# Attention's statistics: whole-tile transposition one slot later, and stores from ScalarE's transfer queue

## The chip, the cores and the metric

The kernel runs on one core of a Trainium2 chip. The metric is the device time of one execution in microseconds, as the median of the runs. A program of one core has its five engines: TensorE (PE in the profile; its weight loads are PEld), VectorE (DVE), ScalarE (ACT), GpSimd (POOL) and SyncE (SP), whose queue issues the transfers (SPq).

## The reference

Two layers of a decoder trunk, for 1024 positions of 1024 channels in float32. Layer 0 mixes by dilated attention, layer 1 by a gated linear recurrence; each mixer and each MLP after it closes with a layer norm of `alpha * x + y`. The change is in the attention alone:

```
for (window, dilation) in ((128,1), (512,4), (2048,16)):      # three groups g, 16 heads of 64
    q, k = rotary(proj[g, 0]), rotary(proj[g, 1])
    s = q k^T / 8 inside the dilated window;  m = max(s);  p = exp(s - m);  l = sum(p)
    o_g = (p / l) v;   lse_g = m + log(l)
o = sum over g of softmax(lse)_g * o_g;   y = o @ w_out
```

So each group leaves an output and two statistics, m and l, for each position and head, and the three groups are mixed with weights made of these.

## The kernel before

Heads go in eight pairs `pr` (two heads of 64 rows fill 128 partitions), and the 24 units (pair, group) in twelve `groups` of two: the first unit `a = 0`, the second `a = 1`. The projections of a group are 21 products (`product(n)`, twelve matmuls `pmm` in float32 parts, lines 666 to 668), and the work of the units before is laid between them by hand: `fill[slot]` holds what is called behind product `slot`, and the tables `ROPES`, `OFFS`, `STATS` and `MIX` give the slots, counted from `base`. Inside this stage the order of TensorE and VectorE is that of the code (`in_order`); ScalarE's and SyncE's order is made by the scheduler, from the same sequence. After the last product the rest goes as `lists` into the output projection (`outproj_ln`), where a scheduler orders all engines: there L183 to L185 are its matmuls on `aoh`, `aol` (the split attention output) and `woh`, `wol` (the split weights, loaded as `wor`); attention outputs of earlier pairs were spilled to DRAM and come back as `onr`.

A unit's core has six steps, two slots apart: `qk` (scores `s`; VectorE adds the mask and takes the row maximum, ScalarE the exponential `p` with its sum), `vtrans` (`vpt`, copied to `vn`), `ptr` (transposes `ppt` of `p`, copied to `pts`) and `pv` (output bank `o`, copied to `og`). The banks of PSUM: three `mm` for products, two `s`, two `pt` for `vpt`, `ppt`, `mpt` and `fb` in turn, one `o`.

Each unit's maxima and sums go into a tile `stats` of 128 x 32 (statistic, head, block of 128 queries). `combine_tr` has three steps, at the slots of `STATS`: TensorE transposes that tile (`mpt`, L564) and ScalarE copies the 32 rows out (`sr`, L566); SyncE stores them in DRAM (`mdram`, L569); SyncE loads them back into `ml` in the layout in which the three groups meet (L575 for dilation 1, L578 otherwise). When a pair's last group, dilation 1, is there, `combine` makes the weights (`mn`, `ml`, L592 to L609), split into `fh` and `fl`, and sends them with six transfers into six rows of `frow` (L616); `combine_mul` spreads them over the partitions with a matmul (`fb`, L626) and VectorE multiplies `og` by it (L627) and adds the groups (L629, L630).

Of the kernel before, what the change touches and what calls it, by code (L numbers as in the profile page):

```python
# [9 lines left out]
F32 = mybir.dt.float32  # L10
F32R = mybir.dt.float32r
U8 = mybir.dt.uint8
AF = mybir.ActivationFunctionType
# [3 lines left out]
P = 128  # L17
# [5 lines left out]
DIL = (1, 4, 16)  # L23
# [29 lines left out]
RESIDENT = 2  # L53
MIX = ((20, 21, 21, 24, 25, 30, 31, 32, 33, 33, 34, 35, 35, 36),
       (30, 31, 33, 34, 35, 37, 38, 39, 41, 41, 42, 42, 42, 43))
STATS = ((12, 13, 15), (21, 22, 24))
ROPES = ((-5, -3, -3, -1, 1, 2), (5, 7, 7, 9, 11, 11))
ROPES0 = ((-5, -2, -1, 2), (-4, 0, 1, 4))
OFFS = ((1, 3, 5, 7, 9, 11), (10, 12, 14, 16, 18, 20))
# [3 lines left out]
def trunk_kernel(  # L63
# [24 lines left out]
    nc = tc.nc  # L88
    cp = ctx.enter_context(tc.tile_pool(name="cp", bufs=1))
# [6 lines left out]
    def U(name, dt=F32):  # L96
        return up.tile([P, 1024], dt, name=name, tag="u")

    def bank(tag, name):
        return ps.tile([P, 512], F32, name=name, tag=tag, bufs={"mm": 3, "s": 2, "pt": 2, "o": 1}[tag])  # L100

    def small(shape, name, bufs=4, dt=F32):
        return sp.tile(shape, dt, name=name, tag=name, bufs=bufs)

    act = nc.scalar.activation
# [21 lines left out]
    ident = cp.tile([P, P], F32, name="ident")  # L127
# [194 lines left out]
    def attention(pre, hc):  # L322
# [120 lines left out]
        sel = cp.tile([P, NG * P], F32R, name="bsel")  # L443
        frow = U("frow", F32R)
        mdram = dp.tile([NPAIR, NG, 2, 2, S], F32, name="mdram")

        def constants():
            nc.sync.dma_start(cosT, cos_t)
            nc.sync.dma_start(sinT, sin_t)
            nc.sync.dma_start(mask, masks)  # L450
# [11 lines left out]
        def nat(ap, g):  # L462
            d = DIL[g]
            return ap if d == 1 else ap.rearrange("p (n r) -> p n r", r=d)

        def rope(e, g, nm):
            rot = U("rot")
            for b4 in range(4):
                o = (b4 ^ 1) * 32
                nc.sync.dma_start(rot[b4 * 32:b4 * 32 + 32, :], e[o:o + 32, :])  # L470
            qT = U(nm)
            nc.vector.tensor_mul(cls(qT, g), nat(e, g), nat(cosT, g))
            return qT, (lambda: nc.vector.tensor_mul(rot, rot, sinT),
                        lambda: nc.vector.tensor_add(cls(qT, g), cls(qT, g), nat(rot, g)))
# [84 lines left out]
                [lambda: pv(6), lambda: pv(7)],  # L559
            ]  # L560

        def combine_tr(pr, g, sS, ml):
            pt = bank("pt", "mpt")
            nc.tensor.transpose(pt[:32, 0:P], sS.rearrange("p w a b -> p (w a b)"), ident)  # L564
            sr = small([32, P], "sr", 2)
            act(sr, pt[:32, 0:P], AF.Copy)  # L566
            yield
            md = mdram[pr, g]
            nc.sync.dma_start(md.rearrange("w h (b q) -> (w h b) q", q=P), sr)  # L569
            yield  # L570

            d = DIL[g]
            for w in range(2):
                if d == 1:
                    nc.sync.dma_start(ml[:, w, 0, :], md[w].rearrange("h (i n) -> (h i) n", n=P))  # L575
                else:
                    for h in range(2):
                        nc.sync.dma_start(  # L578
                            ml[8 * h:8 * h + 8, w, g, :].rearrange("i (r n) -> i r n", r=d),
                            md[w, h].rearrange("(r i n) -> i r n", r=d, i=8))  # L580
            yield

        def combine(pr, ml):
            def cv(tl, g):
                d = DIL[g]
                return tl if d == 1 else tl.rearrange("p (r n) -> p n r", r=d)

            m = ml[:, 0]
            l = ml[:, 1]
            v = nc.vector  # L590
            mn = small([16, P], "mn", 1)
            v.tensor_tensor(nat(mn, 1), nat(m[:, 0], 1), cv(m[:, 1], 1), op=ALU.min)  # L592
            v.tensor_tensor(nat(mn, 2), nat(mn, 2), cv(m[:, 2], 2), op=ALU.min)
            for g in range(NG):
                v.tensor_sub(cv(m[:, g], g), nat(mn, g), cv(m[:, g], g))
            act(m, m, AF.Exp)
            yield
            v.tensor_mul(l, l, m)
            den = mn
            v.tensor_add(nat(den, 1), nat(l[:, 0], 1), cv(l[:, 1], 1))  # L600
            v.tensor_add(nat(den, 2), nat(den, 2), cv(l[:, 2], 2))
            yield
            v.reciprocal(den, den)
            for g in range(NG):
                v.tensor_mul(nat(l[:, g], g), cv(m[:, g], g), nat(den, g))

            fh = wp.tile([P, 512], F32R, name="fh", tag="p")[:16, :NG * P].rearrange("p (g t) -> p g t", t=P)
            fl = wp.tile([P, 512], F32R, name="fl", tag="pts")[:16, :NG * P].rearrange("p (g t) -> p g t", t=P)
            act(fh, l, AF.Copy)  # L609
            yield  # L610
            v.tensor_sub(fl, l, fh.bitcast(F32))
            yield
            for g in range(NG):
                for i, f in enumerate((fh, fl)):
                    r = 4 * g + 2 * i
                    nc.sync.dma_start(frow[r:r + 2, :].bitcast(F32).rearrange("h (i t) -> h i t", t=P),  # L616
                                      f[:, g, :].bitcast(F32))
            yield

        def combine_mul(pr, og, hb):  # L620

            c = slice(hb * 512, hb * 512 + 512)
            acc = og[0]
            for g in GORD:
                fb = bank("pt", "fb")
                nc.tensor.matmul(fb, sel[:, g * P:(g + 1) * P], frow[:, c], start=True, stop=True)  # L626
                nc.vector.tensor_mul(og[g][:, c], og[g][:, c], fb)  # L627
                yield
            nc.vector.tensor_add(og[2][:, c], og[2][:, c], og[1][:, c])  # L629
            nc.vector.tensor_add(acc[:, c], acc[:, c], og[2][:, c])  # L630
            yield
            if hb:
                if pr < SPILL[0]:
                    nc.sync.dma_start(ond[0, pr], acc)
                    oN.append(ond[0, pr])
                else:
                    oN.append(acc)
            yield
# [4 lines left out]
        def at(slot, f):  # L643
            fill.setdefault(slot, []).append(f)

        ep, acc, part = {}, {}, {}
        ml, ogs = {}, {}
# [58 lines left out]
        def unit_work(gi, a, base):  # L706

            pr, g = groups[gi][a]
            if pr not in ml:
                ml[pr] = small([16, 2, NG, P], "ml", 1)  # L710
                ogs[pr] = [None] * NG
            sS = small([P, 2, 2, 8], "stats", 3)

            adds = {}

            def rope_of(t):
                res[a, t], adds[t] = rope(ep.pop((gi, a, 0 if t == 1 else 1)), g, "qT" if t == 0 else "kT")

            def begin():
                ogs[pr][g] = U("og")  # L720
                p = pieces(pr, g, res.pop((a, 0)), res.pop((a, 1)), ep.pop((gi, 2, a)), ogs[pr][g], sS)
                for f in p[0]:
                    f()
                work.extend(p[1:])

            work = []
            later = [lambda: [f() for f in work.pop(0)] for _ in range(5)]
            trs = combine_tr(pr, g, sS, ml[pr])
            stats = [lambda: next(trs, None)] * 3
            mix = []  # L730
            if g == GORD[-1]:
                steps = combine(pr, ml[pr])
                mix = [lambda: next(steps, None)] * 5
                for hb in range(2):
                    muls = combine_mul(pr, ogs[pr], hb)
                    mix += [lambda muls=muls: next(muls, None)] * (4 + hb)
            return adds, rope_of, [begin] + later, stats, mix
# [23 lines left out]
        for n in range(len(seq)):  # L761
            gi, i, j = seq[n]
# [26 lines left out]
            if n % 21 == 14:  # L789
# [3 lines left out]
                for a in range(2):  # L793
                    adds, rope_of, core, stats, mix = work[a]
# [9 lines left out]
                    for k, f in enumerate(core):  # L804
                        at(base + UNIT0 + OFFS[a][k], f)
                    for k, f in zip(STATS[a], stats):
                        at(base + k, f)
# [9 lines left out]
        (ra, ca, sa, _), (rb, cb, sb_, mx) = tail  # L817
        done = [f for n in sorted(fill) for f in fill[n]]
        mine = [[ra[0]], [rb[0], rb[1]], [ra[1]], [ca[0], rb[2]], [ca[1]], [cb[0]], [ca[2]], [cb[1]], [ca[3]], [cb[2]],
                [ca[4]] + sa, [cb[3]], [ca[5]], [cb[4]] + sb_, [cb[5]], mx[:1], mx[1:3], mx[3:5], [],  # L820
                mx[5:7], mx[7:10], mx[10:]]
        lists = [done[k:k + 1] + (mine[k] if k < len(mine) else []) for k in range(max(len(done), len(mine)))]
        return oN, lists
# [661 lines left out]
    def hgrn(xs, late, consts, pre, gw):  # L1485
# [103 lines left out]
        for hd in range(8):  # L1589
# [66 lines left out]
            if hd == 0:  # L1656
                new = [[]] + new
            pend = [(pend[i] if i < len(pend) else []) + (new[i] if i < len(new) else [])
                    for i in range(max(len(new), len(pend)))]
# [9 lines left out]
    pr = Out(w_attn_out, "a", 0)  # L1669
    hc = []  # L1670
    oN, fill = attention(pr.pre_steps, hc)
    xf, late = outproj_ln(pr, oN, fill, lambda t: x[t * P:(t + 1) * P, :],
                          ln_mix_g[0], ln_mix_b[0], x1d)
# [3 lines left out]
    pr = Out(w_hgrn_out, "h", 1)  # L1677
# [81 lines left out]
```

## Time and profile before

| | us |
|---|---|
| median of 3 runs | 2845.02 (2842.76 to 2846.17) |
| the profiled execution | 2844.54 |
| its span, first to last instruction | 2842.8 |
| TensorE busy | 2772.0 |
| VectorE busy | 2068.6 |
| ScalarE busy | 1449.2 |
| mean granted clock of TensorE | 0.996 |

In a row of a timeline stand start, duration, engine, line, operation, tile written and tiles read, and in brackets how long the engine was idle before it and what ended that. Matmuls overlap, so the price of one in TensorE's stream is the distance from its start to the next start, not its duration. In a row of waits stand the total, the number and the longest one. In a row of a tile's instructions stand the least, median and greatest duration in ns. Attention's products run from about 14 to 970 us, the rest of its units until about 1065 us, inside the output projection.

### The profile page before, as it was taken

Reading aid. Unit: us, or ns where it says so; the run is one execution under the profiler, and the core shown is the slowest. Engines: PE = TensorE matmul, PEld = TensorE weight load, DVE = VectorE, ACT = ScalarE, POOL = GpSimd, SP = SyncE. Lnnn points to the kernel's source line nnn. Section 1 sums busy time; section 2 is a strip of 40 time slices with the busy share of each in tenths; the row PEclk is TensorE's granted clock in tenths of the full one; section 3 lists DMA queues with packets and bytes.
Section 4 is the critical chain, followed back from the end, with each engine's and each line's share of the span. In section 5 each row is a group of like instructions: output and inputs, shape, how many; then the busy total and the mean of one; then the engine's idle time right before and its main releaser. Section 6 shows DMA issues by size and latency. Waiting matters only on the chain. (4 is left out here: it accounts for less than half of the span.)

```text
span 2842.8 us, 40144 instructions
## 1 busy us (share of the span) xinstructions
PE 2772.0 (98%) x14280; PEld 2229.9 (78%) x14280; DVE 2068.6 (73%) x3830; ACT 1449.2 (51%) x3105; POOL 122.7 (4%) x67
## 2 busy tenths in 40 slices
PE   8999999999999989999999999999999999999998
PEld 6777777777777767888878887787787788878887
DVE  7768777777777767786686876565667787678677
ACT  5555555555555555544454434555553545454433
POOL 0000000000000003100000011111102200000000
PEclk9999999999999999999999999999999999999999
DMA  7766665766667523464494752101132455475654
GB/s 288 252 200 195 185 206 172 216 198 206 193 194 219 166 87 133 145 226 156 158 320 126 263 177 90 38 31 60 55 117 81 149 204 174 159 271 189 222 175 132
DMA packets 204936, 485.27 MB, mean 171 GB/s; under 512 B 29376, under 2 KB 43712, under 8 KB 204736
## 3 DMA queue, kind: packets, MB, share of 16 engines
q1 hardware_dynamic: 204736, 482.72, 51.5%
q8 instruction: 112, 1.84, 0.3%
q14 instruction: 88, 0.72, 0.1%
HBM read 362.82 MB, written 94.24 MB: 161 GB/s over the span
## 5 line engine op out<-in xcount | busy, mean ns | idle before, releaser
L666 PE MATMUL pmm<-xh,H 128*128 128x512 f32 x1008 | 407.6, 404 | 13.0 <-ACT H L432 8.9
L668 PE MATMUL pmm<-xh,H 128*128 128x512 f32 x1008 | 395.7, 393 | 0.1
L667 PE MATMUL pmm<-xl,H 128*128 128x512 f32 x1008 | 395.6, 392 | 0.0
L666 PEld LDWEIGHTS pmm<-xh,H 128*128 128x128 f32 x1008 | 190.9, 189 | 53.3 <-ACT H L432 8.9
L668 PEld LDWEIGHTS pmm<-xh,H 128*128 128x128 f32 x1008 | 190.2, 189 | 42.3 <-DVE H L440 0.8
L667 PEld LDWEIGHTS pmm<-xl,H 128*128 128x128 f32 x1008 | 191.0, 189 | 36.6
L514 ACT ACTIVATE p<-p,stats 128x128 f32<-128x128 f32 (+1 forms) x384 | 168.3, 441 | 93.6 <-DVE stats L511 92.2
L1260 PE MATMUL pdy<-dT,dS 128*128 128x512 f32 x512 | 199.2, 389 | 0.0
L1263 PE MATMUL pdy<-dT,dS 128*128 128x512 f32 x512 | 199.2, 389 | 0.0
L1264 PE MATMUL pdy<-dT,dS 128*128 128x512 f32 x512 | 199.2, 389 | 0.0
L511 DVE CUSTOM_DVE_ANT_0 p<-s,mask 128x128 f32<-128x128 f32 (+1 forms) x384 | 113.3, 348 | 67.7 <-PE s L500 58.4
L137 ACT ACTIVATE dS<-dr 128x512 fp32r<-128x512 f32 x192 | 119.5, 622 | 73.2 <-PE pdy L1264 36.6
L171 PE MATMUL pmm<-f0nh,wh 128*128 128x512 f32 x384 | 153.2, 399 | 0.0
L173 PE MATMUL pmm<-f0nh,wl 128*128 128x512 f32 x384 | 149.9, 390 | 1.6 <-DVE wl L138 1.6
L172 PE MATMUL pmm<-f0nl,wh 128*128 128x512 f32 x384 | 149.7, 390 | 0.0
L138 DVE TENSOR_TENSOR dS<-dr,dS 128x512 fp32r<-128x512 f32 x192 | 136.2, 710 | 15.8 <-ACT dS L137 13.9
L214 POOL TENSOR_TENSOR z<-z,bB 128x1024 f32<-128x1024 f32 x24 | 58.5, 2442 | 1680.8 <-ACT z L213 1676.7
L527 ACT ACTIVATE pts<-ppt 128x256 f32<-128x256 f32 (+1 forms) x192 | 85.4, 474 | 62.0 <-PE ppt L524 59.8
L137 ACT ACTIVATE dT<-hold 128x512 fp32r<-128x512 f32 x128 | 80.0, 625 | 69.9 <-DVE hold L1239 28.8
L1073 ACT ACTIVATE H<-wc 128x512 fp32r<-128x512 f32 x128 | 77.2, 625 | 73.5 <-DVE wc L1066 44.0
L1263 PEld LDWEIGHTS pdy<-dT,dS 128*128 128x128 f32 x512 | 96.1, 188 | 20.1
L1260 PEld LDWEIGHTS pdy<-dT,dS 128*128 128x128 f32 x512 | 96.1, 188 | 19.8
(395 smaller groups left out, 6950.3 us busy)
## 6 DMA issues: line engine op xcount, KB each, us to landing
xh<-xtd SPq DMA_DIRECT2D x110, 512.0 KB
xl<-xtd SPq DMA_DIRECT2D x110, 512.0 KB
dr<-hd SPq DMA_DIRECT2D x192, 256.0 KB
dr<-in_w_down_dram SPq DMA_DIRECT2D x128, 256.0 KB
rot<-e SPq DMA_DIRECT2D x192, 128.0 KB
wa<-in_w_up_dram SPq DMA_DIRECT2D x48, 512.0 KB
wb<-in_w_attn_dram SPq DMA_DIRECT2D x36, 512.0 KB
wa<-in_w_attn_dram SPq DMA_DIRECT2D x33, 512.0 KB
```

Source lines behind the costliest of these rows:

```text
L137: act(hi, raw, AF.Copy)
L138: nc.vector.tensor_sub(lo, raw, hi.bitcast(F32))
L171: nc.tensor.matmul(o, wh[:, k], xs.h(k), start=k == 0, stop=False)
L172: nc.tensor.matmul(o, wh[:, k], xs.l(k), start=False, stop=False)
L173: nc.tensor.matmul(o, wl[:, k], xs.h(k), start=False, stop=k == NK - 1)
L514: act(p[:, h, :n], p[:, h, :n], AF.Exp, bias=sS[:, 0, h, b:b + 1], scale=-1.0, accum_out=sS[:, 1, h, b:b + 1])
L666: nc.tensor.matmul(o, wh, hi[k // 2][:, c], start=begin and k == 0, stop=False, skip_group_check=True)
L667: nc.tensor.matmul(o, wh, lo[k // 2][:, c], start=False, stop=False, skip_group_check=True)
L668: nc.tensor.matmul(o, wl, hi[k // 2][:, c], start=False, stop=end and k == 3, skip_group_check=True)
L1260: nc.tensor.matmul(o[q], h, T_[:, L], start=begin, stop=False, skip_group_check=True)
L1263: nc.tensor.matmul(o[q], h, T_[:, R], start=False, stop=False, skip_group_check=True)
L1264: nc.tensor.matmul(o[q], l, T_[:, L], start=False, stop=end, skip_group_check=True)
```

## The change

`stats` becomes one tile of 128 x 128 for the whole run, with four slots of 32 columns that the units use in turn; GpSimd clears it once. `combine_tr` transposes the whole tile (128 columns in place of 32) and copies the 32 rows of its slot, at partitions `q0` and up. The three steps are one slot later in `STATS`, and in the lists behind the last product the first step has a place of its own, the other two stand one list later (unit b's first step one place earlier in its list). The store comes from ScalarE's transfer queue. For dilation 1 two transfers go from `sr` straight into `ml`, and nothing goes to DRAM; for the other two groups the loads into `ml` stay with SyncE. Of the six rows of `frow`, the three of `fh` are issued by ScalarE, the three of `fl` by SyncE.

```diff
-STATS = ((12, 13, 15), (21, 22, 24))
+STATS = ((13, 14, 16), (22, 23, 25))
...
+        allS = cp.tile([P, P], F32, name="stats")
+        nc.gpsimd.memset(allS, 0.0)
...
-        def combine_tr(pr, g, sS, ml):
+        def combine_tr(pr, g, slot, ml):
             pt = bank("pt", "mpt")
-            nc.tensor.transpose(pt[:32, 0:P], sS.rearrange("p w a b -> p (w a b)"), ident)
-            sr = small([32, P], "sr", 2)
-            act(sr, pt[:32, 0:P], AF.Copy)
+            nc.tensor.transpose(pt[:, 0:P], allS, ident)
+            q0 = slot * 32
+            sr = small([P, P], "sr", 2)
+            act(sr[q0:q0 + 32], pt[q0:q0 + 32, 0:P], AF.Copy)
             yield
             md = mdram[pr, g]
-            nc.sync.dma_start(md.rearrange("w h (b q) -> (w h b) q", q=P), sr)
+            d = DIL[g]
+            if d == 1:
+                for w in range(2):
+                    nc.scalar.dma_start(ml[:, w, 0, :], sr[q0 + 16 * w:q0 + 16 * w + 16])
+            else:
+                nc.scalar.dma_start(md.rearrange("w h (b q) -> (w h b) q", q=P), sr[q0:q0 + 32])
             yield
 
-            d = DIL[g]
-            for w in range(2):
-                if d == 1:
-                    nc.sync.dma_start(ml[:, w, 0, :], md[w].rearrange("h (i n) -> (h i) n", n=P))
-                else:
+            if d > 1:
+                for w in range(2):
                     for h in range(2):
                         nc.sync.dma_start(
...
-                for i, f in enumerate((fh, fl)):
+                for i, (f, eng) in enumerate(((fh, nc.scalar), (fl, nc.sync))):
                     r = 4 * g + 2 * i
-                    nc.sync.dma_start(frow[r:r + 2, :].bitcast(F32).rearrange("h (i t) -> h i t", t=P),
-                                      f[:, g, :].bitcast(F32))
+                    eng.dma_start(frow[r:r + 2, :].bitcast(F32).rearrange("h (i t) -> h i t", t=P),
+                                  f[:, g, :].bitcast(F32))
...
-            sS = small([P, 2, 2, 8], "stats", 3)
+            slot = (2 * gi + a) % 4
+            sS = allS[:, slot * 32:slot * 32 + 32].rearrange("p (w a b) -> p w a b", w=2, a=2)
...
-                [ca[4]] + sa, [cb[3]], [ca[5]], [cb[4]] + sb_, [cb[5]], mx[:1], mx[1:3], mx[3:5], [],
+                [ca[4]] + sa[:1], sa[1:] + [cb[3]], [ca[5]], sb_[:1] + [cb[4]], sb_[1:] + [cb[5]], mx[:1], mx[1:3], mx[3:5], [],
```

The lines of the changed kernel are two to nine higher than before: `mpt` is L566, `sr` L569, the direct transfer L575, the store L577, `frow` L621, `fb` L631.

On TensorE, around the transposition of a first unit (pair 0, dilation 1), before:

```order
L668 MATMUL pmm<-xh,H 128x512
L539 MATMUL o<-pts,vn 64x128 x8
L524 MATMUL ppt<-ident,p 128x128 x8
L564 MATMUL mpt<-ident,stats 32x128
L666 MATMUL pmm<-xh,H 128x512
```

and now, twelve `pmm` rows further on:

```order
L673 MATMUL pmm<-xh,H 128x512
L566 MATMUL mpt<-ident,stats 128x128
L502 MATMUL s<-kT,qT 128x128 x4
L490 MATMUL vpt<-ident,vT 128x128 x8
L671 MATMUL pmm<-xh,H 128x512
```

The transposition has moved from behind the unit's last `ppt` to behind the next product, where the second unit's scores and `vpt` follow it.

On ScalarE at the same place, before (`e` is a product's copy, `H` a weight's):

```order
L527 ACTIVATE pts<-ppt 128x512 x2
L566 ACTIVATE sr<-mpt 32x128
L697 ACTIVATE e<-pmm 128x512
L514 ACTIVATE p,stats<-p,stats 128x128 x4
L489 ACTIVATE vn<-vpt 128x512 x2
L432 ACTIVATE H<-wc 128x512
L547 ACTIVATE og<-o 128x512
```

and now:

```order
L529 ACTIVATE pts<-ppt 128x512 x2
L702 ACTIVATE e<-pmm 128x512
L569 ACTIVATE sr<-mpt 32x128
L575 DMA ml<-sr 16x128
L516 ACTIVATE p,stats<-p,stats 128x128 x4
L491 ACTIVATE vn<-vpt 128x512 x2
L432 ACTIVATE H<-wc 128x512
L575 DMA ml<-sr 16x128
L549 ACTIVATE og<-o 128x512
```

The copy `sr` stands behind the next product's copy, and the two issues stand ahead of the exponentials and of `og`. Where a pair's weights go out (the next group's second unit), ScalarE now has:

```order
L614 ACTIVATE fh<-ml 16x384
L569 ACTIVATE sr<-mpt 32x128
L621 DMA frow<-fh 2x8x128
L694 ACTIVATE e<-pmm 128x512
L577 DMA mdram<-sr 32x128
L621 DMA frow<-fh 2x8x128
L432 ACTIVATE H<-wc 128x512
L552 ACTIVATE og<-o 128x8x64
L621 DMA frow<-fh 2x8x128
```

Four issues stand there among the copies; before there was none.

On VectorE, at the end of attention (last pair; `wol` and `aol` are low parts of the output projection's operands), before:

```order
L138 TENSOR_TENSOR aol<-onr,aoh 128x512
L629 TENSOR_TENSOR og<-og 128x512
L630 TENSOR_TENSOR og<-og 128x512
L138 TENSOR_TENSOR wol<-wor,woh 128x512 x2
L592 TENSOR_TENSOR mn<-ml 16x128
L593 TENSOR_TENSOR mn<-mn,ml 16x128
L595 TENSOR_TENSOR ml<-mn,ml 16x128
L595 TENSOR_TENSOR ml<-mn,ml 16x32x4
L595 TENSOR_TENSOR ml<-mn,ml 16x8x16
```

and now:

```order
L597 TENSOR_TENSOR mn<-ml 16x128
L634 TENSOR_TENSOR og<-og 128x512
L138 TENSOR_TENSOR aol<-onr,aoh 128x512
L632 TENSOR_TENSOR og<-og,fb 128x512
L598 TENSOR_TENSOR mn<-mn,ml 16x128
L635 TENSOR_TENSOR og<-og 128x512
L600 TENSOR_TENSOR ml<-mn,ml 16x128
L138 TENSOR_TENSOR wol<-wor,woh 128x512
L600 TENSOR_TENSOR ml<-mn,ml 16x32x4
L138 TENSOR_TENSOR wol<-wor,woh 128x512
L600 TENSOR_TENSOR ml<-mn,ml 16x8x16
```

The first step on `ml` has moved ahead of the adds of the pair before, and the others are mixed with the `wol` steps, the last still behind both.

More of the change, by code (lines that the diff above doesn't have):

```diff
@@ L727, in unit_work @@
             later = [lambda: [f() for f in work.pop(0)] for _ in range(5)]
-            trs = combine_tr(pr, g, sS, ml[pr])
+            trs = combine_tr(pr, g, slot, ml[pr])
             stats = [lambda: next(trs, None)] * 3
```

## The prediction

> **What bounds the kernel now.** I read the page first, then the waits of TensorE (PE), then the timeline around each instruction that the diff moves, then the end of the attention stage on all queues.
>
> ```profile
> span 2842.8 us, 40144 instructions
> PE 2772.0 (98%) x14280; PEld 2229.9 (78%) x14280; DVE 2068.6 (73%) x3830; ACT 1449.2 (51%) x3105; POOL 122.7 (4%) x67
> ```
>
> TensorE is busy for 98% of the span; only its own instruction time, or the 70.8 us in which it isn't busy, can shorten the run. VectorE (DVE) and ScalarE (ACT) matter only where TensorE waits for them. In the waits of TensorE between 90 and 1000 us, which is the attention stage, two rows belong to the transposition that the diff moves (`mpt`), and one row of SyncE's queue to the store behind it:
>
> ```profile
> PE mpt L564 <- ACT pts L527: 3.5, 13, 0.3
> PE mpt L564 <- DVE og L627: 1.4, 3, 0.5
> SPq L569 <- ACT sr L566: 149.5, 21, 13.7
> ```
>
> So 4.9 us of the stage's idle time stand before `mpt`: it needs one of the two `pt` banks, and ScalarE hasn't emptied the one before. No wait of TensorE in this window is for a transfer, so SyncE's 149.5 us behind `sr` cost nothing there.
>
> **Part 1: the transposition one slot later.** The price of a thing in TensorE's stream is best read from start to start. The first, one typical and the last of the 21 transpositions between 120 and 945 us, then the same numbers of transposes (four, eight) with a product right behind them and no `mpt`, then the one `mpt` that already stands behind a product:
>
> ```profile
> 119.09 1.11 PE L524 MATMUL ppt<-ident,p 128*128 128x128 f32 x4
> 120.25 0.40 PE L564 MATMUL mpt<-ident,stats 128*32 128x128 f32 x1
> 120.30 0.78 PE L666 MATMUL pmm<-xh,H 128*128 128x512 f32 x1
> ...
> 236.77 0.66 PE L524 MATMUL ppt<-ident,p 128*128 128x128 f32 x4
> 237.69 0.28 PE L564 MATMUL mpt<-ident,stats 128*32 128x128 f32 x1 [0.26 <-ACT pts L527]
> 237.73 0.49 PE L666 MATMUL pmm<-xh,H 128*128 128x512 f32 x1
> ...
> 942.67 1.09 PE L524 MATMUL ppt<-ident,p 128*128 128x128 f32 x8
> 944.01 0.28 PE L564 MATMUL mpt<-ident,stats 128*32 128x128 f32 x1 [0.25 <-ACT pts L527]
> 944.05 0.49 PE L666 MATMUL pmm<-xh,H 128*128 128x512 f32 x1
> ```
> ```profile
> 110.26 0.66 PE L524 MATMUL ppt<-ident,p 128*128 128x128 f32 x4
> 110.68 0.48 PE L666 MATMUL pmm<-xh,H 128*128 128x512 f32 x1
> ...
> 207.10 1.09 PE L488 MATMUL vpt<-ident,vT 128*128 128x128 f32 x8
> 207.94 0.48 PE L666 MATMUL pmm<-xh,H 128*128 128x512 f32 x1
> ...
> 981.46 0.39 PE L185 MATMUL pmm<-woh,aol 128*128 128x512 f32 x1
> 981.69 0.27 PE L564 MATMUL mpt<-ident,stats 128*32 128x128 f32 x1
> 981.80 0.60 PE L488 MATMUL vpt<-ident,vT 128*128 128x128 f32 x4
> ```
>
> Four transposes lead to the product after 0.42 us without `mpt` and 0.96 with it; eight after 0.84 and 1.38: the step costs 0.54 us. Over the 21, worked out so: seven behind eight transposes 0.54 to 0.60 (4.0 together), six behind four 0.54 (3.3), three with the VectorE wait 0.74 (2.2), three that met no wait 0.11 (0.3), the first two 0.80 and 0.33 (1.1). Sum 10.9 us. In the order the step now stands behind the twelve matmuls of a product, as at 981.69, where it costs 0.11 us. By then the banks have had a product's time, some 2.8 us, to be emptied. 21 x 0.11 = 2.3 us. Bounds of one: 0.11, and 0.54 if the wait comes along. I take 0.11, since that row is the same step in the same kind of place. **Net -8.6 us.**
>
> The transposition reads the whole 128x128 tile, so it waits for the last statistics of all units written ahead of it; one slot after a unit's last exponentials these are done, and the order shows it waiting only for a `pts` copy. Its weight load has 128 columns, not 32; the eight transposes above load 128 too, at 0.105 us each, so this is in the 0.11.
>
> **What is late next.** Where the step is a first unit's, the second unit's `vpt` transposes follow, and their second four now need the bank that `sr` empties.
>
> ```profile
> 206.13 0.39 PE L668 MATMUL pmm<-xh,H 128*128 128x512 f32 x1
> ...
> 206.56 0.60 ACT L697 ACTIVATE e<-pmm 128x512 f32<-128x512 f32 x1 [2.51 <-PE pmm L668]
> ```
>
> ScalarE copies `e` at 206.56 to 207.16, then `sr` (0.27 us, below) to about 207.45. The second four would start at 207.10 + 0.11 + 0.42 = 207.63. It fits, by 0.2 us, so zero; one more copy of 0.6 us ahead of `sr` would cost 0.4 us at each of 11 places, 4.4 us: the upper bound.
>
> **Part 2: transfers issued by ScalarE.** 16 stores to `mdram`, 16 direct ones into `ml` and 24 of `frow`. The trace has no transfer issued by ScalarE; SyncE's are the nearest rows:
>
> ```profile
> L566 ACT ACTIVATE sr<-mpt x24: 249/267/270, 120.7 to 1039.8; 32x128 f32<-32x128 f32 x24
> L569 SPq DMA_DIRECT2D mdram<-sr x24: 317/328/1198, 121.0 to 1040.0; - x24
> L575 SPq DMA_DIRECT2D ml<-mdram x16: 312/375/418, 205.5 to 1041.9; - x16
> L616 SPq DMA_DIRECT2D frow<-fh x24: 610/626/712, 242.4 to 1055.5; - x24
> ```
>
> 16 x 0.328 + 16 x 0.375 + 24 x 0.626 = 26.3 us on ScalarE's queue, in which exponentials, `pts`, `e`, `og` and `H` copies stand behind them. It is busy 51% of the time, and what follows the bursts (four issues, 2.2 us, in slots 22 to 26) is an `og` copy whose bank TensorE wants back six slots later, and copies for products two slots off. So nearly all lies beside TensorE's work. Bounds: 0 and 26.3 us; I take +1.0, near the lower end, since the evictions that TensorE waits for closely (`pts`) don't follow a burst in the order. Each issue also waits for an older transfer on its semaphore; all that I followed back were issued a slot or more before. SyncE loses 56 issues and the waits for `sr`: worth nothing, as no TensorE wait there is for a transfer.
>
> The Trainium skill (DMA: Bandwidth & Descriptors, "Issuing engines are not separate DMA queues") says that issuing from several engines saves only the sequencer's issue time, usually small beside the transfer. By it the move would be worth nothing; the sum has a loss of 1.0 instead, from ScalarE's own queue.
>
> **Part 3: the end of attention.** Here a chain counts: the last unit's statistics, the factors, `fb`, `og`, the output projection.
>
> ```profile
> 1044.18 0.39 PE L185 MATMUL pmm<-woh,aol 128*128 128x512 f32 x1
> 1048.16 0.79 PE L183 MATMUL pmm<-woh,aoh 128*128 128x512 f32 x1 [3.59 <-ACT aoh L137]
> 1048.75 0.63 PE L184 MATMUL pmm<-wol,aoh 128*128 128x512 f32 x1
> ...
> 1054.30 0.40 PE L185 MATMUL pmm<-woh,aol 128*128 128x512 f32 x1
> ...
> 1058.28 0.70 PE L626 MATMUL fb<-frow,bsel 128*128 128x512 f32 x2 [0.83 <-DMA frow<-fh]
> ```
> ```profile
> 1046.16 0.87 DVE L595 TENSOR_TENSOR ml<-mn,ml 16x128 f32<-16x128 f32 x3
> ```
> ```profile
> 1047.07 0.52 ACT L596 ACTIVATE ml<-ml 16x384 f32<-16x384 f32 x1 [0.36 <-DMA onr<-ond]
> 1047.50 0.61 ACT L137 ACTIVATE aoh<-og 128x512 fp32r<-128x512 f32 x1
> ```
> ```profile
> 1041.49 0.79 SPq L575 DMA_DIRECT2D ml<-mdram  x2
> ...
> 1052.41 0.63 SPq L616 DMA_DIRECT2D frow<-fh  x1
> ...
> 1056.17 0.61 SPq L616 DMA_DIRECT2D frow<-fl  x1
> ```
>
> TensorE stops for 3.59 us and then runs 13 matmuls 0.427 us apart ((1054.30 - 1048.75)/13) where 0.23 is usual (981.46 to 981.69): 2.5 us more. The stop ends with `aoh<-og`, which on ScalarE stands behind the exponential of `ml`, and that behind VectorE's L595. The change lets `ml` land earlier (issued at about 1038 for 1041.49), but in the new order VectorE does the same two `og` products, two adds, `aol`, two `wol` and `mn` steps ahead of that exponential, and ScalarE has one `aoh<-onr` copy (0.6 us) more between it and `aoh<-og`. I walk it to about 1047.5 against 1048.16: -0.6 us. After it `frow` goes out on two queues, three by three; the six in a row take 1056.17 + 0.61 - 1052.41 = 4.4 us, half is 2.2, of which the later start of the `fl` rows and two `aol` steps that now stand behind `fb` take most back: another -0.4. **-1.0 us**, between +3 (VectorE held by a late `ml`) and -6.1 (stop and slow clock both gone).
>
> **Sum**, against the profiled execution's 2844.54 us: 2844.5 - 8.6 + 1.0 - 1.0 = 2835.9. The median of the runs is 2845.02, 0.5 above; so 2836 us, -0.3%.
>
> **Rivals.**
> (a) The stop at 1044 us goes, and with it the slow clock: -6.1 in place of -1.0, 2831 us. For it: the `wor`, `onr` and `ml` transfers that ScalarE waited for come sooner. Against: VectorE's chain. The Trainium skill (TensorE: Matmul & The Clock Gate, "HAM oscillation") names idle gaps over some 3.4 us as what halves TensorE's clock; the trace agrees (3.59 us, then 0.427 us), so by it a stop that gets only 0.2 us shorter would already save the 2.5 us.
> (b) Half the gain comes back as waits for banks or for ScalarE (`vpt` behind `sr`, 4.4 us): 2841 us, within 0.2% of before.
> (c) Slower: ScalarE stalls at an issue until an older transfer has landed, and `pts` and the exponentials are late for the next transposes. It costs time once ScalarE is over two slots late, and turns the sum at 14.3/22 = 0.65 us of new TensorE wait for each unit (8.6 lost, 5.7 more for 0.2%); SyncE's single waits reach 13.7 us, so a stuck one could. About 2852 us. Against: the older transfers lie well back.
> (d) The step isn't later at all: the order excludes it.
>
> **Chances.** Forecast 0.50, (a) 0.15, (b) 0.26, (c) 0.09. A measurement of this kernel tells 0.2% (5.7 us) from no change: the forecast and (a) are faster, 0.65; (b) the same, 0.26; (c) slower, 0.09. From 2829.5 (below (a)) to 2844 (past (b)) lies over 8 in 10.
>
> **What would show it.** Right: no `mpt` row among TensorE's waits, `mpt` 0.11 us behind the last matmul of a product, the stage some 8 us shorter by 1000 us. Part 1 wrong: waits of `vpt` for `sr`. Part 2 wrong: TensorE's waits for `pts`, `e` or `og` grow, or ScalarE idles behind transfers. Part 3 wrong: a stop near 1040 us under 3 us, or over 5.

## The result and the profile after

| | before | after |
|---|---|---|
| median, nine runs each on the same chip (us) | 2845.84 (2842.29 to 2846.41) | 2835.93 (2833.36 to 2837.94) |
| the profiled execution (us) | 2844.54 | 2833.53 |
| its span (us) | 2842.8 | 2831.5 |

The changed kernel takes 0.9967 of the time, 95% interval 0.9958 to 0.9976: 9.9 us less. The forecast was 2836.0 us.

The page after, its line of engines (us busy, share of the span, instructions):

```profile
PE 2765.8 (98%) x14280; PEld 2228.6 (79%) x14280; DVE 2068.7 (73%) x3830; ACT 1450.0 (51%) x3105; POOL 122.9 (4%) x68
```

The instruction counts of TensorE, VectorE and ScalarE are those of before. TensorE still sets the time, so the gain has to be stream time and waits of TensorE. Its waits after, between 90 and 985 us (total, number, longest):

```profile
PE ppt L526 <- DVE og L632: 3.0, 6, 0.8
PE ppt L526 <- ACT pts L529: 2.8, 6, 0.5
PE o L541 <- ACT og L552: 2.1, 1, 2.1
PE pmm L183 <- DVE vT L706: 0.8, 1, 0.8
```

These rows stand in the profile before with the same numbers. The two `mpt` rows that stood among them (3.5 and 1.4 us) are gone, and no new row has come.

The transposition in its new place, a first unit's and a second unit's, from the timeline of TensorE:

```profile
203.99 0.39 PE L673 MATMUL pmm<-xh,H 128*128 128x512 f32 x1
204.22 0.27 PE L566 MATMUL mpt<-ident,stats 128*128 128x128 f32 x1
204.42 0.72 PE L502 MATMUL s<-kT,qT 64*128 64x128 f32 x8
...
237.79 0.39 PE L673 MATMUL pmm<-xh,H 128*128 128x512 f32 x1
238.02 0.27 PE L566 MATMUL mpt<-ident,stats 128*128 128x128 f32 x1
238.05 0.48 PE L671 MATMUL pmm<-xh,H 128*128 128x512 f32 x1
238.37 0.39 PE L672 MATMUL pmm<-xl,H 128*128 128x512 f32 x1
```

It starts 0.23 us behind the last matmul of the product, with no bracket for a wait. From that matmul to the other unit's `s` it is 0.43 us (0.32 without a transposition, 206.13 to 206.45 in the trace before), and to the next product 0.26, where two matmuls of a product stand 0.23 apart. The second matmul of that product comes another 0.32 us later, again in place of 0.23, so the price at a second unit's place is spread over two distances.

The difference of the two profiled executions, 11.0 us, put together from distances between marks that both have:

| from, to | before | after | change |
|---|---|---|---|
| start to the first wait for `og`, near 118 us | 118.5 | 118.7 | +0.2 |
| to the first product on `aoh` | 855.4 | 846.1 | -9.3 |
| to the first `lnpt` (end of attention) | 111.9 | 111.6 | -0.3 |
| to the first `hpt` of layer 1 | 711.5 | 710.0 | -1.5 |

From there to the last store both take 1042.1 us. The last row isn't the change's work, for no line there was touched, and 1.55 us of the second aren't either: the granted clock fell behind a wait in the profile before and, by chance, not in the one after (last section). In a second profile of the changed kernel (`after_again`) it fell there too, and the second row is 847.7 us: 7.7 less than before. A distance without such a place is that from the second to the twenty-first transposition: 786.79 us before, 779.15 after. That is 7.64 us for 19 of the steps, 0.40 us each. This distance, called the stage below, is the finest ruler of the case: the changed kernel has 779.15 and, profiled again, 779.16 us.

At the end of attention the stop of TensorE is still there, and longer than the 3.59 us of before:

```profile
1033.21 0.39 PE L185 MATMUL pmm<-woh,aol 128*128 128x512 f32 x1
1038.46 0.69 PE L183 MATMUL pmm<-woh,aoh 128*128 128x512 f32 x1 [4.86 <-ACT aoh L137]
...
1040.84 0.80 PE L185 MATMUL pmm<-woh,aol 128*128 128x512 f32 x1 [0.83 <-DVE aol L138]
...
1047.89 0.61 PE L631 MATMUL fb<-frow,bsel 128*128 128x512 f32 x2
```

What was bought is at 1047.89: no wait for `frow`, where before there were 0.83 us. What was paid is at 1040.84: a wait as long for `aol`, which was not there before.

### The profile page after: what moved, and what is told of

The parts are those of the page before. It is cut to its first block, busy times and chain, and to the rows that moved or that the text cites. A ratio compares the mean times of both kernels' runs of the same rounds, so it can differ in the third digit from the quotient of the medians.

```text
span 2831.5 us, 40028 instructions
## 1 busy us (share of the span) xinstructions
PE 2765.8 (98%) x14280; PEld 2228.6 (79%) x14280; DVE 2068.7 (73%) x3830; ACT 1450.0 (51%) x3105; POOL 122.9 (4%) x68
```

## Experiments

Theory T: the place of the transposition in TensorE's stream, and there the wait for a `pt` bank, makes the gain. Rival Q: the transfers make it. Times are medians beside runs of the kernel before on the same chip, with the ratio to these and its 95% interval.

**The later slots alone, in the kernel before.**

```diff
-STATS = ((12, 13, 15), (21, 22, 24))
+STATS = ((13, 14, 16), (22, 23, 25))
```

> The kernel before with the later slots alone (32 columns, all transfers from SyncE through DRAM, the old lists at the end). Theory T (the place of the transposition in TensorE's stream makes the gain): 8 to 10 us below the kernel before, 2836 to 2838 us, and no wait of TensorE for a bank at the transposition. Rival Q (the gain comes from the transfers: ScalarE's queue, the way without DRAM, SyncE's relief): no change, 2845 us.

Measured: 2836.84 us, ratio 0.9970 (0.9959 to 0.9982). The stage takes 779.87 us; what it has over the changed kernel's 779.15 comes at one place, a wait of 0.38 us for a weight (`H`). One table of the diff gives the stage's gain, all but that wait, and Q falls. This kernel transposes 32 columns and the changed one 128: it is 0.53 us ahead of the changed kernel at the first transposition and 0.50 at the tenth, so in the new place the whole tile costs nothing.

**The old slots in the changed kernel** (the table back, all else as changed).

> The changed kernel with the old slots (12, 13, 15 and 21, 22, 24), all else as changed. T: the gain is gone, 2844 to 2847 us, and the rows of the transposition behind pts and og copies are back among TensorE's waits (about 5 us); a 128-column weight load in that place may add up to 0.03 us at each of 21 places, 0.6 us. Q: it stays near 2836 us.

Measured: 2845.25 us, ratio 0.9999 (0.9990 to 1.0007). The waits of TensorE in the stage have their old rows again:

```profile
PE mpt L566 <- ACT pts L529: 3.7, 14, 0.3
...
PE mpt L566 <- DVE og L632: 1.4, 3, 0.5
```

The whole tile can be priced here: this kernel falls behind the one before by 0.33 us from the third transposition to the sixteenth (1.85 to 2.18 us), 0.025 us a place. Without the slots the rest of the change is worth nothing.

**Every transfer back on SyncE** (whole tile, later slots and lists stay).

```diff
-            if d == 1:
-                for w in range(2):
-                    nc.scalar.dma_start(ml[:, w, 0, :], sr[q0 + 16 * w:q0 + 16 * w + 16])
-            else:
-                nc.scalar.dma_start(md.rearrange("w h (b q) -> (w h b) q", q=P), sr[q0:q0 + 32])
+            nc.sync.dma_start(md.rearrange("w h (b q) -> (w h b) q", q=P), sr[q0:q0 + 32])
...
-                for i, (f, eng) in enumerate(((fh, nc.scalar), (fl, nc.sync))):
+                for i, (f, eng) in enumerate(((fh, nc.sync), (fl, nc.sync))):
```

> The changed kernel with every transfer back on SyncE and dilation 1 again through DRAM; whole tile, later slots and the new lists stay. T: as the changed kernel, 2834 to 2838 us; only the end of attention may differ, by 3 us either way. Q: 2845 us. Of the prediction's terms, ScalarE's 56 issues (+1.0 us, bounds 0 to 26.3) would show here as a gain of so much in the stage up to 965 us.

Measured: 2837.3 us, ratio 0.9971 (0.9959 to 0.9982). It stands 1.88 us behind the changed kernel at the first transposition and 1.92 at the tenth: ScalarE's queue costs nothing there and gives nothing. Then one wait for `H` of 0.76 us, at 514.84, makes it 2.99. Four of the twelve profiles have a single wait of this kind (0.38 to 1.30 us), three of them at the same matmul, and neither kernel that is compared has one; these three cost some 0.3 us more than they lasted (0.38 cost 0.7 above), the one of 1.30 us, with the old slots, did not. Why it comes was not tried.

**Four more stores for each unit on ScalarE's queue.**

```diff
+            for x in range(4):
+                nc.scalar.dma_start(xdram[pr, g, x].rearrange("w h (b q) -> (w h b) q", q=P), sr[q0:q0 + 32])
             yield
 
             if d > 1:
```

> The changed kernel with four further stores of sr to DRAM after each of the 24 first ones, all issued by ScalarE: 96 more issues, at 0.314 us each 30 us more on its queue. What they store is not read. If ScalarE's issues are hidden (the prediction took 1.0 of 26.3 us; the changed kernel's stage shows about 0): 0 to 1.5 us over the changed kernel, 2836 to 2837.5 us. Rival C (ScalarE stands behind older transfers at its issues and pts and p come late): over 5.7 us more, up to 30, 2842 to 2866 us, with TensorE's waits for pts and p grown.

Measured: 2835.56 us, ratio 0.9970 (0.9958 to 0.9981). The added issues, by tile (least, median, greatest in ns), and TensorE's waits in the stage:

```profile
L580 ACTq DMA_DIRECT2D xdram<-sr x96: 308/432/1164, 123.0 to 1030.4; - x96
```
```profile
PE ppt L527 <- DVE og L635: 3.0, 6, 0.8
PE ppt L527 <- ACT pts L530: 2.8, 6, 0.5
```

96 x 0.432 = 41 us more on ScalarE's queue, and the stage takes 779.18 us against 779.15. The wait for `pts` is 2.8 us in both. Rival (c) of the prediction had the right place to look and no price there.

**The old slots, with a bank that is free.**

```diff
-STATS = ((13, 14, 16), (22, 23, 25))
+STATS = ((12, 13, 15), (21, 22, 24))
...
-            pt = bank("pt", "mpt")
+            pt = bank("s", "mpt")
```

> The changed kernel with the old slots, but the transposition writes one of the two s banks instead of a pt bank, so that it has no pts or og copy to wait for in its old place; all else as changed. Theory B (of the 0.54 us of the old place, 0.26 is the wait for the bank and about as much the stream that has to fill again; only 0.11 is the transposition): nearly all the gain comes back without the later slot, 2836 to 2839 us, no bank wait at the transposition. Rival P (the place behind the transposes costs 0.5 us whatever the bank): 2844 to 2847 us.

Measured: 2833.04 us, ratio 0.9962 (0.9950 to 0.9975). The stage takes 778.32 us, 0.8 under the changed kernel's. In the old place, behind eight transposes:

```profile
200.56 1.09 PE L526 MATMUL ppt<-ident,p 128*128 128x128 f32 x8
201.49 0.27 PE L566 MATMUL mpt<-ident,stats 128*128 128x128 f32 x1
201.52 0.48 PE L671 MATMUL pmm<-xh,H 128*128 128x512 f32 x1
```

From `ppt` to the product it is 0.96 us, where the kernel before had 1.38 with the transposition and 0.84 without: 0.12 us instead of 0.54. So it was never the place: it was the bank. The wait that the trace gave as 0.26 us cost 0.42 in the distance of starts. Run again beside the changed kernel on one chip:

> The old slots with an s bank once more. Theory B (only the bank wait made the old place dear): within 1.5 us of the changed kernel beside it. If it is 2 us or more below, the old place is the better one once it has a free bank, since the statistics leave a slot earlier and no transposition stands ahead of a second unit's s.

> The changed kernel once more, beside the next two on one chip: 2834 to 2838 us, 0.9958 to 0.9976 of the kernel before. Its profile shows what changes of itself from run to run (the first wait for H near 9 us, the granted clock behind the short stops).

Measured: 2834.58 us (0.9965, 0.9953 to 0.9978) for the s bank, with a stage of 778.32 us again, against 2835.12 us (0.9966, 0.9954 to 0.9978). By the medians the two ways are equal within what can be told, though the stage is 0.8 us shorter with the `s` bank in both of its profiles. No kernel's median here is measurably lower than the changed one's.

**No transposition at all.** ScalarE fills `sr` from a tile of ones, so the three groups are weighted alike, and the weights depend on no statistics.

```diff
-            pt = bank("pt", "mpt")
-            nc.tensor.transpose(pt[:, 0:P], allS, ident)
...
-            act(sr[q0:q0 + 32], pt[q0:q0 + 32, 0:P], AF.Copy)
+            act(sr[q0:q0 + 32].rearrange("p (o c) -> p o c", o=2), onesT[q0:q0 + 32].rearrange("p (o c) -> p o c", o=1).broadcast_to([32, 2, 64]), AF.Copy)
```

> The changed kernel without the 24 transpositions: ScalarE fills sr from a constant tile of ones, so the three groups are weighted alike. What it gains is what the transposition still costs in its new place. T: 21 x 0.02 to 0.11 us, 0.4 to 2.3 us below the changed kernel, 2833.5 to 2835.5 us. Rival H (the price only moved, to the second unit's vpt and s and to the product behind them): 8 to 11 us below, 2825 to 2828 us.

Measured: 2839.9 us, ratio 0.9981 (0.9972 to 0.9990), a miss for both: slower than the changed kernel. The experiment had a side effect. Nothing holds the copies into `sr` back, so the scheduler put nine of them, with stores, into the first 32 us, and ScalarE stands there until each buffer's transfer is through:

```profile
13.44 0.30 ACT L569 ACTIVATE sr<-ones 32x128 f32<-32x128 f32 x1 [4.70 <-DMA mdram<-sr]
...
21.97 0.31 ACT L569 ACTIVATE sr<-ones 32x128 f32<-32x128 f32 x1 [6.57 <-DMA ml<-sr]
```
```profile
PE pmm L671 <- ACT H L432: 27.2, 1, 27.2
```

TensorE's first wait is 27.2 us in place of 9.5, and the first `s` comes 13.8 us late. The parts can still be read. From the first `s` to the first product on `aoh` it takes 875.4 us, with two waits that the changed kernel doesn't have: 0.59 us for `H` and 0.2 for `p`, which cost some 0.9 and 0.6. The changed kernel takes 876.8. So the 21 transpositions still cost about 3 us. Matmul set against matmul around each place, the changed kernel loses 0.11 to 0.17 us at twenty of them and 0.37 at the last, 3.1 us in all; against the kernel before, which has no transposition at these places, the same comparison gives the same numbers. That is above T's 2.3 us, and far below the 8 of H. And from there to the first `lnpt` it takes 103.5 us where the changed kernel has 111.6: with the weights early, the end of attention is 8.1 us shorter. That is about what the chain behind the last statistics costs (three transpositions at the end are missing too).

**The end of attention: the split of pair 6 ahead of the exponential.**

```diff
             nc.vector.tensor_add(acc[:, c], acc[:, c], og[2][:, c])
+            if pr >= SPILL[0] and hb == 0:
+                pre.__self__.raw[pr] = acc
+                pre.__self__.split_k(pr, 0)
             yield
```

(and no second time in the output projection)

> The changed kernel with one thing moved at the end of attention: the split of the first half of pairs 6 and 7 (aoh, aol from og) is written right behind the sum of that half, so that aoh of pair 6 stands ahead of the exponential of ml on ScalarE, which held it in the changed kernel while TensorE stood still for 4.86 us. Theory S (the stop and the slow clock behind it can go by themselves): 4 to 6 us below the changed kernel, 2830 to 2832 us. Rival K (the chain from the last statistics to frow sets the end): the stop is gone near 1034 us, but TensorE waits for frow ahead of fb instead, 3 to 5 us, and the time is 2834 to 2837 us.

Measured: 2836.3 us, ratio 0.9972 (0.9961 to 0.9984): the time of K. In the waits of TensorE from 1030 to 1060 us the one stop of 4.86 us is gone, and two others stand in its stead, at 1038.9 (3.2 us) and 1047.6 us (5.0 us):

```profile
PE pmm L183 <- ACT aoh L137: 5.2, 2, 5.0
PE pmm L183 <- DVE z L942: 3.5, 2, 3.2
```

They are not at `fb`, where the expectation of K had put them, but their sum is larger; first `aoh` product to first `lnpt` is 114.0 us against 111.6.

**The same, with the chain ahead in the scheduler's order.**

```diff
-                mix = [lambda: next(steps, None)] * 5
+                def step():
+                    if gi == len(groups) - 1:
+                        with tc.high_priority(offset=200):
+                            next(steps, None)
+                    else:
+                        next(steps, None)
+                mix = [step] * 5
```

(and likewise for the three steps of `combine_tr`)

> split_early, and the steps of the last pair's statistics (transposition, sr, the weights from mn to frow) are given a higher priority in the scheduler's order: sr stands ahead of the og copy on ScalarE, and fewer other steps of VectorE between mn and the exponential of ml (two in place of five). Theory K (the chain from the last statistics to frow sets the end): what the chain gets shorter, 2 to 4 us, the end of attention gets shorter, 2832 to 2834 us. Rival D (ml arrives late behind the bulk loads of z, wor and onr, whatever the order of the engines): 2835 to 2837 us, VectorE idle ahead of mn for longer than 1.4 us.

Measured: 2835.09 us, ratio 0.9966 (0.9953 to 0.9978): no gain. VectorE, the first step of the weights:

```profile
1032.35 0.38 DVE L597 TENSOR_TENSOR mn<-ml 16x128 f32<-16x128 f32 x1 [4.15 <-DMA onr<-ond]
```

Behind the last transposition `sr` and `mn` both come 0.5 us earlier, but from `sr` to `mn` it is 5.0 us as in the changed kernel: VectorE idles 4.15 us ahead of `mn` for `ml` (1.38 in the changed kernel; the load `onr` that the row names is not read by `mn`). From the last transposition to the first `frow` transfer it is 15.0 us instead of 16.3, and the stage's end to `lnpt` 111.1 us instead of 111.6 to 112.7. That `ml` is late behind the loads of `z`, `onr` and `wor`, as D says, agrees with the idle time but was not shown by a run that takes these loads away.

## Why the prediction was right, point by point

**Part 1 (-8.6 us): right in cause, 0.9 us too large.** With the clock low behind the wait for `og` in both, the part is 7.7 us. About 3.1 us are left where 2.3 were worked out, so some 10.8 went where the prediction had 10.9. The 0.11 us of a place came from one row, read to the next start only; to the matmul after it, a second unit's place costs 0.12 too (0.26 and 0.32 in place of 0.23 twice), and the mean of the 21 is 0.15. The first of the old rows, 0.80 us, was read behind the wait for `og`, where the clock had fallen: with the clock low in both kernels, the wait and the next unit's `s` stand 5.72 us apart before and 5.62 after, so the step's move bought 0.1 us there. The cause, a bank that ScalarE hasn't emptied, was argued in the prediction; the run with an `s` bank shows it.

The margin of 0.2 us for `vpt` behind `sr` was enough at ten of the eleven places, and at one it was not:

```profile
who waited for it (us, times):
  PEld vpt L490: 1.9, 6
```
```profile
938.21 0.62 ACT L432 ACTIVATE H<-wc 128x512 fp32r<-128x512 f32 x1
938.73 0.24 ACT L569 ACTIVATE sr<-mpt 32x128 f32<-32x128 f32 x1
939.03 0.42 PEld L490 LDWEIGHTS vpt<-ident,vT 128*128 128x128 f32 x4 [0.25 <-ACT sr L569]
```

Those six are weight loads (PEld). At five of them no matmul was late. At the last, 939.03 us, an `H` copy stands ahead of `sr`, the case that the prediction priced at 0.4 us, and the matmuls behind came some 0.23 us late.

**Part 2 (+1.0 us): the size was off; it is 0.** The issues by tile:

```profile
L577 ACTq DMA_DIRECT2D mdram<-sr x16: 308/314/367, 123.6 to 1021.5; - x16
L575 ACTq DMA_DIRECT2D ml<-sr x16: 534/580/636, 205.3 to 1027.6; - x16
```
```profile
L621 ACTq DMA_DIRECT2D frow<-fh x24: 617/656/1201, 240.4 to 1043.6; - x24
```

16 x 0.314 + 16 x 0.580 + 24 x 0.656 = 30 us, more than the 26.3 worked out from SyncE's rows, and none of it reached TensorE in the stage, as the run on SyncE alone and the one with 41 us more both show. The rule quoted there, that the choice of the issuing engine is worth little (the Trainium skill, DMA: Bandwidth & Descriptors, "Issuing engines are not separate DMA queues"), agrees with these runs in the stage: 0.0 us.

That SyncE's relief is worth nothing holds for the time, but not for the reason given. The prediction's 149.5 us are the whole run's (131.2 to 1000 us), and its window has a wait of TensorE for `z`, whose load SyncE issued late; in the changed kernel the load goes out 26 us earlier and the wait is gone:

```profile
PE pmm L183 <- DVE z L933: 1.4, 1, 1.4
```
```profile
987.37 1.29 SPq L907 DMA_DIRECT2D z<-in_x_dram  x3
```
```profile
991.17 0.69 DVE L933 SCALAR_TENSOR_TENSOR z<-z,pmm 128x512 f32<-128x512 f32 x1 [2.75 <-DMA z<-in_x_dram]
```
```profile
961.08 2.12 SPq L913 DMA_DIRECT2D z<-in_x_dram  x3
```

Only the three profiles with every transfer on SyncE (before, later slots alone, all back on SyncE) have this wait, 1.4 to 1.6 us. It bought nothing because TensorE only came sooner to the stop at the end of attention.

**Part 3 (-1.0 us): not borne out.** From the first product on `aoh` to `lnpt` it takes 111.6 us in one profile and 112.7 in the other, against 111.9. The walk to the end of the stop was right in the first: counted from the first product on `aoh`, the stop ends 73.57 us on, before it was 74.23, so 0.66 us sooner where the walk had 0.6 (0.15 in the second profile). It is longer, 4.86 us and just under the 5 us that the prediction named as a wrong sign, because TensorE comes to it 1.9 us sooner, 1.4 of them from `z`. The step that failed is the second, 0.4 us from `frow` on two queues: the wait of 0.83 us for `frow` is gone, but 0.83 us for `aol` stand between the stop and `fb`, and from the stop's end to `lnpt` it takes 38.0 us (38.6 in the second profile) in place of 37.7. What kept the stop from ending sooner still is, by the rows below, `ml`, which the walk had landing in good time: VectorE waits before its first step on it, in the second profile by the row's own word for `ml`, and ScalarE's `aoh` stands behind the exponential of `ml`:

```profile
1031.74 0.39 DVE L597 TENSOR_TENSOR mn<-ml 16x128 f32<-16x128 f32 x1 [1.38 <-DMA wor<-in_w_attn_out_dram]
```
```profile
1033.72 0.39 DVE L597 TENSOR_TENSOR mn<-ml 16x128 f32<-16x128 f32 x1 [1.85 <-DMA ml<-sr]
```
```profile
1036.85 0.52 ACT L601 ACTIVATE ml<-ml 16x384 f32<-16x384 f32 x1 [4.01 <-DVE ml L600]
1037.28 0.61 ACT L137 ACTIVATE aoh<-onr 128x512 fp32r<-128x512 f32 x1
1037.80 0.61 ACT L137 ACTIVATE aoh<-og 128x512 fp32r<-128x512 f32 x1
...
1042.14 2.03 ACTq L621 DMA_DIRECT2D frow<-fh x3
1044.22 0.63 ACT L137 ACTIVATE aoh<-onr 128x512 fp32r<-128x512 f32 x1 [2.11 <-DMA frow<-fh]
```

**The sum.** That the forecast meets the median to 0.1 us is luck. By the traces with like clocks the parts are 7.7 us gained, 0, and between 0.3 gained and 0.8 lost, so 7 to 8 us in all; the medians say 9.9, and their interval, 6.8 to 12.0 us, holds both.

**The rivals.** (a) had the right stake: with early weights the end was 8.1 us shorter. But the stop is only where the chain behind the last statistics shows; moving `aoh` out of its way made two new waits. (b) came at one place of eleven, with 0.23 us in place of its 0.4, and otherwise no bank wait replaced the old ones. (c) is excluded for 152 issues in place of 56.

## What to carry to other kernels

Price a small step by the start-to-start distance around it, and when it waits, ask for what: here 0.42 of 0.54 us was a bank that ScalarE had not emptied, and either a later slot or another bank removes it. A transfer's issue on an engine with idle time in every slot costs nothing until a buffer's release waits for the transfer. A stop at the end of a chain is not removed by moving the one instruction it names: find the chain's first late step.

## What was not expected of the hardware

**The slow clock needs no long stop.** In the profile of the last experiment the end of attention has no wait of TensorE above 1.9 us, yet the granted clock (the third number from the end of a row of stretches) is 0.50 for ten microseconds:

```profile
PE pmm L183 <- DVE z L954: 3.3, 2, 1.9
PE pmm L183 <- ACT aoh L137: 1.1, 1, 1.1
```
```profile
1030.00:1040.00 10.00, 7.38 (x43) 5.13 (x42) 7.65 (x17) 4.29 (x8) 0.00 (x0) 1.00 0.53 190
1040.00:1050.00 10.00, 7.21 (x15) 4.30 (x16) 5.90 (x13) 2.41 (x4) 0.00 (x0) 0.50 0.34 110
```

And the same wait does both. In two profiles of the changed kernel, one program, TensorE waits 2.09 us for `og`; behind it the granted clock over ten microseconds is 1.00 in the first and 0.83 in the second:

```profile
118.74 0.66 PE L541 MATMUL o<-pts,vn 128*64 128x128 f32 x8 [2.09 <-ACT og L552]
```
```profile
118.00:128.00 10.00, 9.26 (x61) 7.07 (x61) 3.79 (x16) 7.00 (x20) 0.00 (x0) 1.00 0.72 285
```
```profile
118.67 0.66 PE L541 MATMUL o<-pts,vn 128*64 128x128 f32 x8 [2.09 <-ACT og L552]
```
```profile
118.00:128.00 10.00, 9.33 (x50) 7.29 (x51) 3.42 (x14) 5.91 (x18) 0.00 (x0) 0.83 0.66 254
```

From the wait to the next unit's `s` it is 4.07 us in the first and 5.62 in the second: 1.55 us of chance. In seven of the twelve profiles the clock fell there, before among them. In the feed-forward part a wait of 2.14 us (`lnpt` for `f0nl`) stands in all twelve profiles; in six of them the clock over the twenty microseconds around it is 0.91, before among them, in six 1.00, after among them, and that is the -1.5 of the table above. Two such coins fell well for the profile after, so 11.0 us is too much to claim from it; without them it is some 8.

The Trainium skill (TensorE: Matmul & The Clock Gate, "The HAM clock gate") calls the watched window of 3.4 us free-running, which fits a wait that does both. Its rule "no PE-idle gaps >~3.4 us" ("HAM oscillation") is too mild for these rows: 2.09 us once, or several waits under 1.9 us close together, are enough. So the remark at rival (a), that a stop 0.2 us shorter would already save the slow clock, had no ground.

**A direct transfer costs more to issue than the load it replaces:** 0.580 us for `ml<-sr` on ScalarE against 0.375 for `ml<-mdram` on SyncE before. And three issues of `frow` in a row (2.03 us, quoted above) held ScalarE's next copy back by 2.11 us, while a copy that stood ahead of two `ml<-sr` ran beside them:

```profile
1027.02 0.63 ACT L137 ACTIVATE aoh<-onr 128x512 fp32r<-128x512 f32 x1
1027.03 1.21 ACTq L575 DMA_DIRECT2D ml<-sr  x2
```
